# Three engines held to the order of the program in both mixers of a hybrid diffusion backbone

## The chip, the cores and the metric

One core of a Trainium2 chip runs the whole kernel in one launch. The metric is the device time of that launch in microseconds (us), lower is better. Differences of under about 0.2% (5.4 us) are not told from no change here.

## The reference

Two layers work on 512 tokens of 1024 channels: 256 context tokens and 256 latent tokens. A layer is a half-step SwiGLU, a token mixer, and a second half-step SwiGLU, each wrapped in a modulated post-norm. The mixer is what matters here:

```
p   = u @ w_in                          # z, x, B, C, dt | lx, lg | q, k, v, g, alr | gate
ssd = rms_norm(bidirectional chunked scan of (x, dt, B, C) * silu(z))
lru = (forward + backward linear scan of conv(lx)) * gelu(lg)
gla = rms_norm(bidirectional gated linear attention of (q, k, v)) * silu(g)
y   = (sum over n of sigmoid(gate_n) * (branch_n @ w_branch_n)) @ w_out
```

Latent scans start from the final context state. In layer 1 only latent tokens leave the mixer, so much of its work is on 256 columns (`c0 = TL`).

## The kernel before

**Products.** Activations lie with channels on partitions and tokens along the columns. A float32 product is made of three fp32r matmuls (`mm3`, L372 to L374): activations and weights are each split into a rounded part and a rest. A weight block of 128 x 1024 is loaded by SyncE, ScalarE writes its rounded part (L342), VectorE its rest (L344), both in `split_ahead`. One such block feeds one projection: `proj` (called a step below) issues 24 matmuls into one PSUM bank.

**Foreground and background.** `mixer` goes through two hand-written lists, `ORDER` and `ORDER2`. Their letters are foreground steps: L an LRU pair, S an SSD group (four channel tiles through `chan`, two z tiles), G a gate, M and B merges of a branch, V and Q the GLA projections, D the dt rows, N the SSD norm. The scans are background generators (`lru_batch`, `ssd_dt`, `ssd_group`, `ssd_norm`, `gla_head`). After every projection `pump` advances them by a budget of 5.0 us in layer 0 and 2.5 us in layer 1 (the numbers that they yield), and a `yield None` ends a generator's turn. `need(t)` advances the first generator in the list again and again until `t` is done.

**Chains between engines.** `chan` evicts a projection with a convolution: ScalarE L860, six (or eight) VectorE pieces L869, ScalarE tanh L1413, VectorE L1414. `ssd_group` works two heads at a time: states (L1065, L1072), decay exponents (VectorE L1088, ScalarE L1090 and L1092), state output (L1097, L1100), weights L1108, a GpSimd sum L1111, the product L1118, the rest L1124 to L1132. `ssd_norm` takes eight tiles, each VectorE L1154, ScalarE L903, VectorE L904. `gla_head` ends in L1242 (transposes), L1259 and L1263 (states), L1279 (output), L1287, L1288, L1292, L897, L898, L1298, L1300.

**Who sets the order.** What is written above is the order in which the program emits instructions. The framework then schedules them: it keeps data dependences and, on each engine, places what its own estimates call ready, earlier emitted work first. So before the change any instruction may pass another on its engine. `keep_in_program_order` (used by `pin` for the very first stage and by `table` for table preloads) adds an edge without a wait: the instruction is placed behind everything emitted before it on its engine. SyncE's and GpSimd's instructions carry no such edge before or after.

Of the kernel before, what the change touches and what calls it, by code (L numbers as in the profile page):

```python
# [39 lines left out]
ORDER2 = ("V0 Q0 N Q1 B0 B1 B2 B3 H0 V1 Q2 B4 B5 B6 H1 Q3 B7 F H2 G24 G20 G21 G22 G23 C G25 G26 G27",  # L40
          "V0 Q0 N G00 G01 G02 Q1 B0 G05 B1 V1 B2 H0 B3 Q2 B5 B4 H1 Q3 B6 B7 F H2 G22 C G20 G21 G27 G23 G24 G26 G25")
POOL_HI = (0, 0)
SEG = ((), ())
LOW = 4
BUDGET = (5.0, 2.5)
# [22 lines left out]
class Any:  # L68
    def __getattr__(self, n):
        return self  # L70
# [11 lines left out]
        return False  # L82


class Half:


    def __init__(self, page, o):
        self.page, self.o, self.mate = page, o, None
# [7 lines left out]
class Prog:  # L97
    def __init__(self, tc, aps, wlist=None, seq=None):
        self.dry = tc is None
        self.tc = Any() if self.dry else tc  # L100
        self.nc = self.tc.nc
        self.a = aps if not self.dry else Any()
        self.plan = seq
        self.seq = []
        self.wlist = wlist
# [394 lines left out]
    def prologue(self):  # L500
        nc, a = self.nc, self.a
        self.hp = [self.F() for _ in range(KT)]
        cs = self.F()
        nc.vector.memset(self.ones, 1.0)
        nc.sync.dma_start(cs[:, :16].rearrange("p (k b) -> p k b", b=2), a["cc"])
        nc.scalar.dma_start(self.par[0], a["par"][0])
        self.raw_free += self.once
        self.retired = {id(t) for t in self.once}
        for k in range(KT):
            self.ada_load(k)  # L510
            nc.sync.dma_start(self.hp[k], a["hT"][:, k])
            if not self.dry:
                self.raw_issue(min(NRAW + len(self.once), k + 1))
        nc.vector.memset(self.sst.rearrange("p a b -> p (a b)"), 0.0)
        self.filler()
        nc.scalar.activation(self.sst[:, :, 0:2], cs[:, :16].rearrange("p (k b) -> p k b", b=2), AF.Silu)
        self.fF(cs)
        if not self.dry:
            make_identity(nc, self.ident)
        srow = self.F()  # L520
        nc.vector.tensor_copy(srow[:, 0:16].rearrange("p (b k) -> p k b", b=2), self.sst[:, :, 0:2])
        ps = self.B()
        nc.tensor.transpose(ps[0:16, 0:P], srow[:, 0:16], self.ident)
        nc.scalar.activation(srow[0:16, P:2 * P], ps[0:16, 0:P], AF.Copy)
        self.fB(ps)
        nc.gpsimd.dma_start(self.s_d.rearrange("b (k p) -> (b k) p", p=P), srow[0:16, P:2 * P])
        self.fF(srow)
        nc.vector.memset(self.eps, EPS)
        nc.vector.memset(self.eps4, 4.0 * EPS)
        four = self.ident.rearrange("p (j a c) -> p j a c", a=2, c=32)  # L530
        nc.vector.tensor_tensor(self.sel.rearrange("p (j c) -> p j c", c=2), four[:, :, 0, 0:2], four[:, :, 1, 0:2],
                                op=ALU.add)
        for d in range(2):
            nc.gpsimd.memset(self.gmask[d], 1.0)
            nc.gpsimd.affine_select(out=self.gmask[d], in_=self.gmask[d], pattern=[[1 if d == 0 else -1, P]],
                                    compare_op=ALU.is_ge, fill=0.0, base=0,
                                    channel_multiplier=-1 if d == 0 else 1)
        for c in (64, 128):
            nc.vector.memset(self.rst[c], 1.0)
            nc.vector.memset(self.rst[c].rearrange("p (a b) -> p a b", b=c)[:, :, 0:1], 0.0)  # L540
# [470 lines left out]
    def ssd_group(self, l, g, ys, Bp, Cp, zs, c0):  # L1011
# [31 lines left out]
        for p in range(2):  # L1043
# [35 lines left out]
            for d in range(2):  # L1079
                for i in range(2):  # L1080
                    o = 32 * d + hh[i]
                    act = 2 * d + i in SEG[l]
                    for c in ch:
# [240 lines left out]
    def mixer(self, l):  # L1324
        nc = self.nc
# [5 lines left out]
        self.bg = []  # L1331
        self.ssq = None
        self.split_banks = True
        def gate(n, m):
            pg = self.proj(self.in_specs(l, OFF["gate"] + n * D + m * P), u, c0)
            th = self.Fc(c0)
            nc.scalar.activation(th[:, c0:], pg[:, c0:], AF.Tanh, scale=0.5)
            self.fB(pg)
            return th
# [35 lines left out]
        def merge(n, m, br, th=None):  # L1375
            th = th or eg.pop((n, m), None) or gate(n, m)
            pb = self.proj([("br", l, n, k, m) for k in range(KT)], lambda k: br[k], c0)
            nc.vector.scalar_tensor_tensor(th[:, c0:], th[:, c0:], 1.0, pb[:, c0:], op0=ALU.add, op1=ALU.mult)
            self.fB(pb)
            if m not in mp:  # L1380
                mp[m] = th
            else:
                nc.vector.tensor_tensor(mp[m][:, c0:], mp[m][:, c0:], th[:, c0:], op=ALU.add)
                self.fF(th)
# [48 lines left out]

        self.pool_hi = POOL_HI[l]
        for x in ORDER[l].split():
            i = int(x[1:] or 0)
            if x[0] == "D":
                alr, dtg = dt_rows()
            elif x[0] == "L":
                lru_pair(i)  # L1440
            elif x[0] == "S":
                ssd_start(i)
            elif x[0] == "G":
                eg[divmod(i, 10)] = gate(*divmod(i, 10))
            elif x[0] == "P":
                self.pool_hi = i
            elif x[0] == "R":
                self.need(*bt)
            elif x[0] == "M":
                merge(1, i, lru)  # L1450
# [51 lines left out]
        for x in ORDER2[l].split():  # L1502
            i = int(x[1:] or 0)
            if x[0] == "V":
                v = gla_v(i)
            elif x[0] == "Q":
                gla_proj(i, v)
            elif x[0] == "N":
                self.need(*sg)
                norm = self.start(self.ssd_norm(l, ys, c0, ssd))  # L1510
            elif x[0] == "B":
                self.need(norm)
                merge(0, i, ssd)
            elif x[0] == "H":
                self.need(gh[i])
            elif x[0] == "G":
                eg[divmod(i, 10)] = gate(*divmod(i, 10))
            elif x[0] == "F":
                for t in range(KT):
                    self.fR(*ssd[t])  # L1520
            elif x[0] == "C":
                cv = self.start(self.to_hilo(go, range(6), c0, gla))
# [4 lines left out]
        for m in range(KT):  # L1527
            merge(2, m, gla)
            x = mp[m]
# [4 lines left out]
        for t in range(KT):  # L1534
            self.fR(*gla[t])
        self.split_banks = False
        assert not self.hfree and len(self.rpages) == 2 * len(self.rpairs)
        self.more_slots([], [self.pair(self.rpairs[i:i + 2]) for i in range(0, len(self.rpairs) - 1, 2)])
        self.res_begin(l, 1, 1.0, c0)
# [201 lines left out]
```

## Time and profile before

| | |
|---|---|
| median of 3 runs | 2720.79 us (2719.93 to 2722.16) |
| profiled execution | 2721.23 us, span 2719.4 us |
| TensorE matmul, weight load | 2659.5 us (98%), 2282.7 us (84%) |
| VectorE | 1932.3 us (71%) |
| ScalarE | 1224.6 us (45%) |
| GpSimd | 349.9 us (13%) |

Busy time is the union of an engine's instructions. Ends of matmuls are modelled, so a busy TensorE need not be at its peak. The mixer of layer 0 runs from about 388 to 1209 us of the span, that of layer 1 from about 1945 to 2506 us.

### The profile page before, as it was taken

Reading aid. Unit: us, or ns where it says so; the run is one execution under the profiler, and the core shown is the slowest. Engines: PE = TensorE matmul, PEld = TensorE weight load, DVE = VectorE, ACT = ScalarE, POOL = GpSimd, SP = SyncE. Lnnn points to the kernel's source line nnn. Section 1 sums busy time; section 2 is a strip of 40 time slices with the busy share of each in tenths; the row PEclk is TensorE's granted clock in tenths of the full one; section 3 lists DMA queues with packets and bytes.
Section 4 is the critical chain, followed back from the end, with each engine's and each line's share of the span. In section 5 each row is a group of like instructions: output and inputs, shape, how many; then the busy total and the mean of one; then the engine's idle time right before and its main releaser. Section 6 shows DMA issues by size and latency. Waiting matters only on the chain.

```text
span 2719.4 us, 38650 instructions
## 1 busy us (share of the span) xinstructions
PE 2659.5 (98%) x14869; PEld 2282.7 (84%) x14869; DVE 1932.3 (71%) x3469; ACT 1224.6 (45%) x1757; POOL 349.9 (13%) x296
## 2 busy tenths in 40 slices
PE   9999999999999999999999999999999999999997
PEld 7888897677888888888888888888977898899997
DVE  5888769599986545468887587633698898676654
ACT  4233237863435444433323142332388645575543
POOL 0000132112220000040000130001311112012002
PEclk9999999999999999999999999999999999999999
DMA  7566533134342222235556435532333454343553
GB/s 287 191 189 200 176 121 125 63 100 149 123 145 74 82 86 78 86 101 170 192 193 196 132 133 186 177 117 99 105 111 108 134 173 140 102 147 125 176 190 116
DMA packets 117832, 380.48 MB, mean 140 GB/s; under 512 B 13888, under 2 KB 22352, under 8 KB 117648
## 3 DMA queue, kind: packets, MB, share of 16 engines
q1 hardware_dynamic: 116000, 373.52, 41.8%
q0 software_dynamic: 1504, 4.34, 0.5%
q8 instruction: 116, 1.90, 0.3%
q14 instruction: 68, 0.56, 0.1%
q10 hardware_dynamic: 144, 0.17, 0.0%
HBM read 373.63 MB, written 4.33 MB: 139 GB/s over the span
## 4 chain that ended last, share of the span: by engine, by line
PE 64%; DVE 7%; ACT 3%; issue 2%; DMA 1%; POOL 0%; SPq 0%; DVEq 0%; POOLq 0%; ACTq 0%
PE bank L372 20%; PE bank L373 19%; PE bank L374 19%; PE bank L1279 1%; PE bank L1259 1%; DVE x L869 1%; DVE wl L344 1%; PE bank L1097 1%; PE bank L1065 0%; PE bank L1118 0%; DVE f L669 0%; DVE m1l L344 0%; DVE f L670 0%; DVE x L1108 0%; PE bank L921 0%
## 5 line engine op out<-in xcount | busy, mean ns | idle before, releaser
L342 ACT ACTIVATE wh<-wr 128x1024 fp32r<-128x1024 f32 x388 | 410.2, 1058 | 734.3 <-PE bank L373 526.2
L344 DVE TENSOR_TENSOR wl<-wr,wh 128x1024 fp32r<-128x1024 f32 x388 | 483.5, 1247 | 257.6 <-ACT wh L342 256.2
L488 DVE SCALAR_TENSOR_TENSOR ada_scr<-wr,sb 128x1024 f32<-128x1024 f32 x256 | 316.3, 1236 | 128.6 <-DMA wr<-in_ws_dram 126.0
L372 PE MATMUL bank<-u0h,wh 128*128 128x512 f32 (+1 forms) x660 | 246.3, 375 | 5.3 <-ACT u0h L675 3.8
L372 PE MATMUL bank<-r,wh 128*128 128x512 f32 (+1 forms) x736 | 251.4, 342 | 0.0
L373 PE MATMUL bank<-r,wh 128*128 128x512 f32 (+1 forms) x736 | 249.7, 340 | 0.0
L374 PE MATMUL bank<-r,wl 128*128 128x512 f32 (+1 forms) x736 | 249.6, 339 | 0.0
L373 PE MATMUL bank<-u0l,wh 128*128 128x512 f32 (+1 forms) x660 | 236.0, 358 | 2.1 <-DVE u0l L677 2.0
L374 PE MATMUL bank<-u0h,wl 128*128 128x512 f32 (+1 forms) x660 | 237.3, 360 | 0.4 <-DVE wl L344 0.4
L372 PE MATMUL bank<-u1h,wh 128*128 128x512 f32 (+1 forms) x660 | 234.7, 358 | 0.6 <-ACT u1h L675 0.6
L373 PE MATMUL bank<-u1l,wh 128*128 128x512 f32 (+1 forms) x660 | 234.3, 356 | 0.8 <-DVE u1l L677 0.7
L374 PE MATMUL bank<-u1h,wl 128*128 128x512 f32 (+1 forms) x660 | 234.1, 355 | 0.0
L372 PE MATMUL bank<-u2h,wh 128*128 128x512 f32 (+1 forms) x660 | 233.5, 355 | 0.0
L373 PE MATMUL bank<-u2l,wh 128*128 128x512 f32 (+1 forms) x660 | 233.3, 354 | 0.0
L374 PE MATMUL bank<-u2h,wl 128*128 128x512 f32 (+1 forms) x660 | 232.8, 353 | 0.0
L373 PE MATMUL bank<-u3l,wh 128*128 128x512 f32 (+1 forms) x644 | 228.5, 355 | 1.2 <-DVE u3l L677 1.2
L372 PE MATMUL bank<-u3h,wh 128*128 128x512 f32 (+1 forms) x644 | 228.5, 356 | 0.0
L374 PE MATMUL bank<-u3h,wl 128*128 128x512 f32 (+1 forms) x644 | 228.2, 355 | 0.0
L372 PEld LDWEIGHTS bank<-r,wh 128*128 128x128 f32 x736 | 139.4, 190 | 15.3 <-ACT wh L342 0.2
L374 PEld LDWEIGHTS bank<-r,wl 128*128 128x128 f32 x736 | 139.5, 190 | 14.9
L373 PEld LDWEIGHTS bank<-r,wh 128*128 128x128 f32 x736 | 139.5, 190 | 14.8
L372 PEld LDWEIGHTS bank<-u0h,wh 128*128 128x128 f32 x660 | 125.8, 191 | 28.4 <-issue 5.7
(507 smaller groups left out, 5918.2 us busy)
## 6 DMA issues: line engine op xcount, KB each, us to landing
wr<-in_ws_dram SPq DMA_DIRECT2D x602, 512.0 KB, 3.5
m1r<-in_ws_dram SPq DMA_DIRECT2D x29, 512.0 KB, 3.9
ada<-in_ws_dram SPq DMA_DIRECT2D x16, 512.0 KB, 9.0
x<-acs_d SPq DMA_DIRECT2D x26, 256.0 KB, 3.4
x<-acs_d SPq DMA_DIRECT2D x45, 128.0 KB, 3.8
x<-in_lw_dram SPq DMA_DIRECT2D x16, 256.0 KB, 3.7
sb<-s_d SPq DMA_DIRECT2D x6, 512.0 KB, 5.8
f<-acs_d SPq DMA_DIRECT2D x19, 128.0 KB, 3.8
```

What stands on the lines that cost most here:

```text
L342: self.pin(nc.scalar.activation(hi, raw, AF.Copy))
L344: self.pin(nc.vector.tensor_tensor(lo, raw, hi, op=ALU.subtract))
L372: x = self.pin(nc.tensor.matmul(out, st[0], mv[0], start=start, stop=False, skip_group_check=True))
L373: self.pin(nc.tensor.matmul(out, st[0], mv[1], start=False, stop=False, skip_group_check=True))
L374: self.last_mm = self.pin(nc.tensor.matmul(out, st[1], mv[0], start=False, stop=stop, skip_group_check=True))
L488: nc.vector.scalar_tensor_tensor(self.ada_scr, raw.rearrange("p a b -> p (a b)"), 1.0, self.sb[b], op0=ALU.mult, op1=ALU.mult, accum_out=o ...
L869: nc.vector.scalar_tensor_tensor(ys[:, :, a:z], xs[:, :, a + o:z + o], w(k), ys[:, :, a:z], op0=ALU.mult, op1=ALU.add)
L1097: nc.tensor.matmul(cc(ps, c), cc(Sd[d], c), cc(Cp, c), start=True, stop=True, skip_group_check=True)
L1259: nc.tensor.matmul(ps[:, 0:256], cc(kt[d], a), vv(a), start=True, stop=True)
L1279: nc.tensor.matmul(cc(po[w], c), lh, rh, start=n == 0, stop=n == len(steps) - 1, skip_group_check=True)
```

## The change

Inside `mixer`, from the start of its first projection to the point ahead of the residual stage, every matmul, transpose, activation and vector operation (the names in `OPS`) is given the edge that keeps it behind whatever was emitted before it on TensorE, VectorE or ScalarE. A thin wrapper around the core's engines does this. What is emitted, its operands and its order of emission stay as they were; `ORDER`, `ORDER2` and the budgets are untouched.

```diff
+ORDERED = ("tensor", "vector", "scalar")
...
+class Engine:
...
+    OPS = {"matmul", "transpose", "activation", "tensor_tensor", "tensor_scalar", "scalar_tensor_tensor", "tensor_copy",
+           "tensor_tensor_scan", "reciprocal"}
...
+        def op(*a, **k):
+            x = f(*a, **k)
+            if self.name in self.prog.ordered:
+                self.prog.tc.keep_in_program_order(x)
+            return x
+        return op
...
-        self.nc = self.tc.nc
+        self.ordered = ()
+        self.nc = Any() if self.dry else Core(self)
...
         self.split_banks = True
+        self.ordered = ORDERED
...
         self.split_banks = False
+        self.ordered = ()
```

## Rows read from the trace of the kernel before

**Rows 1.** The page's busy time by engine over the whole span.
```profile
PE 2659.5 (98%) x14869; PEld 2282.7 (84%) x14869; DVE 1932.3 (71%) x3469; ACT 1224.6 (45%) x1757; POOL 349.9 (13%) x296
```

**Rows 2.** Busy time in three stretches (columns: stretch, length, engines, PEclk, DMA, GB/s).
```profile
388.00:514.00 126.00, 118.36 (x574) 93.26 (x573) 99.96 (x185) 92.91 (x128) 29.57 (x25) 0.97 0.32 104
514.00:765.00 251.00, 241.63 (x1188) 196.06 (x1188) 228.29 (x513) 130.08 (x192) 54.88 (x29) 0.99 0.35 115
1967.00:2281.00 314.00, 299.90 (x1812) 255.44 (x1811) 274.17 (x573) 210.86 (x333) 56.57 (x56) 0.98 0.41 133
```

**Rows 3.** TensorE's waits in mixer 0: us in total, times, longest.
```profile
PE bank L921 <- ACT x L1000: 4.9, 1, 4.9
...
PE bank L921 <- ACT x L922: 2.8, 1, 2.8
```

**Rows 4.** ScalarE by line, 514 to 765: busy, mean ns, idle before and releaser.
```profile
L342 ACT ACTIVATE wh<-wr 128x1024 fp32r<-128x1024 f32 x36 | 37.9, 1055 | 43.8 <-PE bank L373 40.5 <-issue 3.3
L1090 ACT ACTIVATE x<-x 128x512 f32<-128x512 f32 x22 | 13.8, 628 | 8.8 <-DVE x L1088 8.1
...
L1413 ACT ACTIVATE x<-x 128x512 f32<-128x512 f32 x15 | 9.4, 629 | 20.9 <-DVE x L869 20.9
...
L1092 ACT ACTIVATE x<-x 128x512 f32<-128x512 f32 x6 | 3.8, 627 | 7.1 <-DMA x<-acs_d 7.1
...
L903 ACT ACTIVATE r<-x 128x512 fp32r<-128x512 f32 x5 | 3.2, 633 | 4.9 <-DVE x L965 4.8
```

**Rows 5.** VectorE by line, 514 to 765.
```profile
L1414 DVE SCALAR_TENSOR_TENSOR x<-x,x 128x512 f32<-128x512 f32 x15 | 10.2, 683 | 0.6 <-ACT x L1413 0.6
...
L946 DVE SCALAR_TENSOR_TENSOR x<-x,x 128x512 f32<-128x512 f32 x8 | 5.3, 687 | 10.8 <-ACT x L941 10.8
...
L904 DVE TENSOR_TENSOR r<-x,r 128x512 fp32r<-128x512 f32 x5 | 3.4, 682 | 0.7 <-ACT r L903 0.7
```

**Rows 6.** Chain of waits, 733 to 757: start, us, what.
```profile
734.64 1.34 PE bank L1065 x12
...
741.43 1.34 PE bank L1097 x12
```

**Rows 7.** Timeline, 841 to 890, VectorE and then ScalarE: start, us, instruction.
```profile
866.09 2.06 DVE L1154 SCALAR_TENSOR_TENSOR x<-x,par,x 128x512 f32<-128x512 f32 x3
...
880.80 0.69 DVE L1288 TENSOR_TENSOR x<-x,x 128x512 f32<-128x512 f32 x1 [0.58 <-ACT x L1287]
...
885.52 1.28 DVE L1298 TENSOR_TENSOR x<-bank,x 128x512 f32<-128x512 f32 x2
886.72 1.40 DVE L1300 SCALAR_TENSOR_TENSOR x<-x,par,x 128x512 f32<-128x512 f32 x2
...
882.71 0.69 ACT L897 ACTIVATE x<-bank,eps 128x512 f32<-128x512 f32 x1 [0.64 <-PE bank L1292]
```

**Rows 8.** Timeline, 2281 to 2324, TensorE and then ScalarE.
```profile
2284.41 1.50 PE L1065 MATMUL bank<-x,x 128*128 128x128 f32 x12
...
2291.30 0.65 PE L1118 MATMUL bank<-x,x 128*64 128x128 f32 x6
...
2311.06 0.42 ACT L903 ACTIVATE r<-x 128x256 fp32r<-128x256 f32 x1 [0.55 <-DVE x L1154]
```

**Rows 9.** Table loads: groups of mixer 0 (370 to 1230), then one load's timeline.
```profile
L232 ACT ACT_TABLE_LOAD x9 | 11.5, 1283 | 0.2
...
L1090 ACT ACT_TABLE_LOAD x1 | 1.3, 1283 | 0.0
...
849.11 1.28 ACT L232 ACT_TABLE_LOAD   x1
850.40 1.16 ACT L1181 ACTIVATE x<-x 128x512 f32<-128x512 f32 x2
```

**Rows 10.** Granted clock (third from last) behind the longest TensorE wait of mixer 0.
```profile
468.00:471.00 3.00, 2.98 (x5) 1.75 (x6) 3.00 (x9) 2.95 (x4) 0.00 (x0) 0.50 0.90 276
471.00:474.00 3.00, 3.00 (x8) 1.81 (x8) 2.64 (x11) 2.96 (x5) 0.00 (x0) 0.61 0.39 150
```

More of the change, by code (lines that the diff above doesn't have):

```diff
@@ L82, in __exit__, with __init__, __getattr__ @@
         return False
+class Engine:
+    OPS = {"matmul", "transpose", "activation", "tensor_tensor", "tensor_scalar", "scalar_tensor_tensor", "tensor_copy",
+           "tensor_tensor_scan", "reciprocal"}
+    def __init__(self, prog, name):
+        self.prog, self.name, self.eng = prog, name, getattr(prog.tc.nc, name)
+    def __getattr__(self, n):
+        f = getattr(self.eng, n)
+        if n not in self.OPS:
+            return f
+        def op(*a, **k):
[4 more added lines that the diff above has]
+        return op
+class Core:
+    def __init__(self, prog):
+        self.nc = prog.tc.nc
+        self.tensor, self.vector, self.scalar = (Engine(prog, n) for n in ("tensor", "vector", "scalar"))
+    def __getattr__(self, n):
+        return getattr(self.nc, n)
 class Half:
@@ L518, in prologue @@
         if not self.dry:
-            make_identity(nc, self.ident)
+            make_identity(nc.nc, self.ident)
         srow = self.F()
```

## The prediction

> **What bounds the kernel now.** Read the page's busy shares first: TensorE is busy 98% of the span, VectorE 71%, ScalarE 45% [rows 1]. That is an average. The change touches the mixers alone, so take the busy times by stretch next [rows 2]. In the SSD part of layer 0 (514 to 765) VectorE works 228.3 of 251 us, in the LRU and SSD part of layer 1 (1967 to 2281) 274.2 of 314: there two engines are nearly full at once, TensorE with 9.4 and 14.1 us idle, VectorE with 22.7 and 39.8. In the LRU part of layer 0 (388 to 514) ScalarE works 92.9 of 126 and TensorE idles 7.6. Then the waits of TensorE: the two largest of layer 0 that name ScalarE are 4.9 and 2.8 us, both in LRU batches [rows 3]. Last, who waits inside the full stretch: VectorE waited 0.6 us in all for the tanh L1413 (15 of them, 0.63 us each) and 0.7 for the rounding L903 [rows 4, 5]. These chains go VectorE, ScalarE, VectorE with nothing between them in the program, so other instructions stand in their gaps now: VectorE's order in the trace is not the program's. TensorE's nearly is: between the state products L1065 and the outputs L1097 lie exactly 24 foreground matmuls, (741.43 - 734.64 - 1.34) = 5.45 us [rows 6], and I take 5.45 for a full-width step and half of it, 2.7, for a step of 256 columns.
>
> **The change part by part.** It adds no instruction and removes none but table loads. What it takes away is the filling of gaps. I went through the emission order and noted where a wait becomes bare.
>
> *1. Chains inside the full stretch of layer 0.* Each of 16 channel tiles: VectorE stands for L1413, 16 x 0.63 = 10.1 us. After it ScalarE does the next weight block, L342, 1.06, while VectorE does L1414, 0.68, and then L344 needs the block: 16 x 0.4 = 6. After a head pair's last L1088 come one L1090 and two L1092 before ScalarE can evict the next projection: 0.63 + 2 x 0.63 = 1.9, for some six pairs 11.3. Five L903, 0.63 each, 3.2 [rows 4, 5]. Together 30.6. The wait of 10.8 for the LRU exponentials stays [rows 5]. VectorE then needs 228.3 + 10.8 + 30.6 = 269.7 in 251: **+19**. Bounds: 0 if VectorE is never more than a step behind where TensorE needs it, +31 if no wait falls into today's idle time. I take the middle value since 12 of today's 22.7 us are not that LRU wait. Behind a standing L1414 are queued L344 of the block two steps on and the next convolution, whose bank and whose weights TensorE waits for.
>
> *2. The same in layer 1.* Most channel tiles are full width: 16 x 0.6 = 9.6; 16 x 0.4 = 6.4; eight pairs at two thirds of 1.9 (L903 is 0.42 on half the columns against 0.63 [rows 4, 8]), 10; eight roundings 3.4: 29.4. 274.2 + 29.4 = 303.6 would fit into 314, but load and budget are uneven: a channel step of 2.7 to 5.45 us carries a weight split, a convolution and 2.5 us of background. Bounds 0 and +29. I take **+10**, a third.
>
> *3. The drain ahead of B0, both layers.* `need(norm)` first runs `gla_head` to its end, then the norm, with no projection between. In layer 0 three norm tiles are emitted between the transposes and L1263; a tile is 0.69 + 0.63 + 0.68 = 2.0 us [rows 4, 5, 7] now that L904 cannot wait beside the next L1154. L1263 waits 6, TensorE has about 2 us of its own there: 4 lost. L1287 (as L903) and L1288 stand bare ahead of L1292: 1.3. After L1292: 0.69 + 0.63 + 1.28 + 1.40 = 4.0, then four tiles, 8.0; the gate and merge of B0 are 10.9 and hide all but 1.1 and the last block's matmuls. About **+7**. In layer 1 five tiles come after L1292, and the gate was done early: two thirds of (4.0 + 5 x 2.0) is 9.3 against a merge of 2.7: 6.6 and the small wait, **+7**. Bounds 0 and +12 each.
>
> *4. The drain at N in layer 1.* `need(*sg)` runs the last pair from L1065 to L1118 with no projection between. In the trace that takes 2284.4 to 2292.0, 7.5 us, and foreground matmuls stand in it [rows 8]. Bare, I take **+6**; bounds: half of 7.5, since about that was foreground, and 7.5. In layer 0 this pair ends before N.
>
> *5. The clock.* After the 4.9 us wait the granted clock is 0.50 for 3 us and 0.61 for the next 3, the lower level of 1.2 GHz for most of it [rows 3, 10]: 1.5 + 1.2 = 2.7 us lost behind a wait of that length. I count two to three more such waits (B0, N): **+6**; bounds -5 (today's drops go) and +12.
>
> *6. Table loads.* Layer 0 has 47 in 13 groups, 1.283 us each [rows 9]. Which functions share a table the trace shows by where no load stands. Counted so in program order there are 35, as each LRU batch then does its sigmoids, roots and exponentials in one piece: 12 x 1.283 = 15.4 us of ScalarE. Six of the 12 lie in the LRU part, where ScalarE ends waits: **-6**; bounds 0 and -15. A load costs its own length only: the next activation starts 850.40 - (849.11 + 1.28) = 0.01 us later [rows 9]. The Trainium skill (ScalarE: Activation LUTs, "What ACT_TABLE_LOAD costs") adds a drain of 1.38 us to each switch, 2.66 together. By it the 12 would give 32 us and the six 16, and the forecast would be 10 us lower; the row shows no drain, so it does not enter.
>
> Everything else I cost at nothing: GLA heads are spread over pumps with `yield None` and VectorE is half idle there; the final merges have no background; SyncE's queue is free as before. If the loads on it slip, wh comes late: two to four steps of lookahead cover that.
>
> Sum: 19 + 10 + 7 + 7 + 6 + 6 - 6 = **+49**. The profiled execution took 2721.2 us (its span 2719.4 and 1.8 around it), 0.4 above the median of the runs: **2770 us**.
>
> **The rivals.**
>
> *A. Faster.* The scheduler works from estimates; TensorE's idle time is partly its misplacement. If VectorE is always within one step of TensorE, parts 1 to 4 vanish. Then ScalarE decides, in the LRU parts: the 7.6 us idle and 3.8 us of clock (0.03 x 126) there, and half of the 14.1 in layer 1, go: -18, **2703**. For it: fewer loads, and the budgets in the program pace the background. Against: VectorE at 91% of the full stretch leaves no room for bare chains. It decides from the point where layer 0's 30.6 us fit into idle time.
>
> *B. No change.* TensorE's order is nearly the program's already [rows 6], and gains in LRU pay for the drains: **2721**. Against: bare waits are on the other two engines.
>
> *C. Lockstep.* All bare waits count, tables gain nothing, drains take their upper bounds: 30.6 + 29.4 + 24 + 7.5 + 12 = 103.5, **2825**. For it: ScalarE's tanh waits for VectorE's convolution and holds the next weight block behind it, and the background products need the pump before.
>
> *D. The order doesn't change,* since scheduled order equals program order: excluded for VectorE and ScalarE by the filled gaps [rows 5].
>
> **How the numbers follow.** Forecast 0.50, its own range 2740 to 2800; C 0.20; A 0.22; B 0.08. A measurement of this kernel tells 0.2% (5.4 us) from no change. So slower 0.70, same 0.08, faster 0.22. The range of 2708 to 2835 leaves out about half of A and a third of C.
>
> **What would show it.** L1414 waits for L1413 by about 0.6 us each in the changed trace, and L904 for L903; the eight L1154 come 2.0 us apart in layer 0. In 514 to 765 the same steps take some 270 us, with VectorE the engine that TensorE waits for. Behind B0 and at N TensorE's granted clock falls to 0.5. The LRU parts get shorter, with 35 loads in layer 0. I am wrong if TensorE's idle time in the mixers shrinks, or if the loss sits in the GLA heads, the merges or a DMA wait.

## The result and the profile after

The changed kernel takes **3006.07 us** (median of 4 runs, 3003.12 to 3008.02) against 2720.36 us before (4 runs): 285.7 us slower, ratio 1.105 (95% interval 1.1033 to 1.1060). The forecast of 2770 had the sign and a sixth of the size, and its range ended at 2835. The profiled execution has a span of 3006.3 us and a mean granted clock of 0.952 (0.992 before).

In the changed kernel a helper issues the wrapped instructions, so the trace shows them all at one line, L101; its rows are read by their tiles. `x<-bank,par 128x512` on ScalarE is L860 or L922, `x<-x` the tanh L1413 (in sums of waits also L1090, L1092 and L1132), `r<-x` the rounding L903, `wh<-wr` the split L342; on VectorE `wl<-wr,wh` is L344, the scans are L956 to L960, and `x<-bank,par,x 128x255` is the convolution. In the experiments' own rows the line numbers are those of before.

The page's busy time of the changed kernel answers to [rows 1]:

```profile
PE 2742.2 (91%) x14869; PEld 2330.8 (78%) x14869; DVE 1954.5 (65%) x3469; ACT 1203.7 (40%) x1740; POOL 316.2 (11%) x296
```

VectorE has the same instructions and ScalarE 17 fewer, all of them table loads; TensorE is busy 83 us longer with the same matmuls, and all three stand more. Next, busy time by stretch, for the stretches in which as many foreground matmuls end as in those of [rows 2] (columns: stretch, length, PE, PEld, DVE, ACT, POOL, granted clock, DMA share, GB/s):

```profile
389.50:560.00 170.50, 133.40 (x575) 100.86 (x573) 110.86 (x190) 84.73 (x117) 26.97 (x29) 0.89 0.26 81
560.00:873.50 313.50, 258.68 (x1189) 205.37 (x1188) 218.95 (x496) 126.92 (x192) 48.82 (x28) 0.89 0.28 88
2114.50:2524.50 410.00, 318.69 (x1813) 267.95 (x1813) 279.00 (x563) 204.92 (x327) 51.58 (x56) 0.87 0.31 100
```

These three are 44.5, 62.5 and 96.0 us longer than before, 203 of the 286 us. TensorE's idle time there rose from 7.6, 9.4 and 14.1 us to 37.1, 54.8 and 91.3, together by 152; its busy time for the same matmuls rose by 15.0, 17.0 and 18.8 us, together 51, and the granted clock fell from between 0.97 and 0.99 to between 0.87 and 0.89. Counted by foreground matmuls done, 16 us more go where layer 1's mixer starts (in what were the 32 us ahead of the third stretch), and 66 us behind the LRU and SSD lists (24 in layer 0, 42 in layer 1).

TensorE's waits in mixer 0 (us in total, times, longest) answer to [rows 3], where the two largest that named ScalarE were 4.9 and 2.8:

```profile
PE bank L101 <- ACT x L101: 52.1, 5, 20.2
PE bank L101 <- DVE x L101: 19.4, 8, 8.0
PE bank L101 <- ACT wh L101: 14.9, 6, 5.1
PE bank L101 <- DVE wl L101: 11.5, 7, 7.0
```

One stand in the timeline shows how it comes about. TensorE first (start, us, instruction, idle time before it and releaser): six rows of LRU gate products (L921), 14.87 us of nothing, the next two.

```profile
604.81 2.73 PE L101 MATMUL bank<-x,x 128*128 128x512 f32 x6
622.41 2.08 PE L101 MATMUL bank<-x,x 128*128 128x512 f32 x2 [14.87 <-ACT x L101]
```

ScalarE in the same time:

```profile
602.04 0.76 ACT L101 ACTIVATE x<-bank,par 128x512 f32<-128x512 f32 x1
608.11 0.63 ACT L101 ACTIVATE x<-x 128x512 f32<-128x512 f32 x1 [5.30 <-issue]
608.64 1.04 ACT L101 ACTIVATE wh<-wr 128x1024 fp32r<-128x1024 f32 x1
614.42 0.63 ACT L101 ACTIVATE r<-x 128x512 fp32r<-128x512 f32 x1 [4.74 <-DVE x L101]
614.96 0.76 ACT L101 ACTIVATE x<-bank,par 128x512 f32<-128x512 f32 x1
618.78 0.63 ACT L101 ACTIVATE x<-x 128x512 f32<-128x512 f32 x1 [3.06 <-DVE x L101]
619.32 1.04 ACT L101 ACTIVATE wh<-wr 128x1024 fp32r<-128x1024 f32 x1
620.38 1.28 ACT L101 ACT_TABLE_LOAD   x1
621.67 1.84 ACT L101 ACTIVATE x<-bank,par 128x512 f32<-128x512 f32 x3
```

And VectorE, a convolution and then one turn of it:

```profile
605.12 2.91 DVE L101 SCALAR_TENSOR_TENSOR x<-bank,par,x 128x255 f32<-128x255 f32 x6
608.77 0.69 DVE L101 SCALAR_TENSOR_TENSOR x<-x,x 128x512 f32<-128x512 f32 x1 [0.74 <-ACT x L101]
609.71 1.23 DVE L101 TENSOR_TENSOR wl<-wr,wh 128x1024 fp32r<-128x1024 f32 x1 [0.26 <-ACT wh L101]
610.86 0.68 DVE L101 TENSOR_TENSOR_SCAN x<-x,x 128x256 f32<-128x256 f32 x1
611.58 0.75 DVE L101 TENSOR_TENSOR_SCAN x<-x,x,x 128x256 f32<-128x256 f32 x1
613.70 0.69 DVE L101 TENSOR_TENSOR x<-x,x 128x512 f32<-128x512 f32 x1 [1.37 <-POOL x L996]
615.09 0.69 DVE L101 TENSOR_TENSOR r<-x,r 128x512 fp32r<-128x512 f32 x1 [0.69 <-ACT r L101]
615.75 2.94 DVE L101 SCALAR_TENSOR_TENSOR x<-bank,par,x 128x255 f32<-128x255 f32 x6
619.45 0.69 DVE L101 SCALAR_TENSOR_TENSOR x<-x,x 128x512 f32<-128x512 f32 x1 [0.76 <-ACT x L101]
```

The background has three PSUM banks, and the fourth product needs one of them back. The sigmoid that empties the first one (L922, 621.67) stands in ScalarE's queue behind two tanh, a rounding and two weight splits, and ScalarE waited 5.30, 4.74 and 3.06 us there for VectorE (the first row names no releaser, but its tanh starts at 608.11, and the convolution that it reads ends at 605.12 + 2.91 = 608.03). VectorE meanwhile takes 10.7 us for one turn (608.77 to 619.45): the background that one pump emits, and one channel's split and convolution. One projection of TensorE is 5.45 us [rows 6]. Before the change such a turn's background could lie where VectorE had room; now every later weight block waits for it. The Trainium skill (PSUM — Partial Sum Buffer, "Engine vs sequencer instructions") calls the queues of ScalarE, VectorE and GpSimd strict FIFO and has matmuls start in program order; these rows agree for ScalarE, VectorE and TensorE: nothing passes a standing instruction.

Last, whom ScalarE waits for. Before, from 388 to 765:

```profile
ACT wh L342 <- PE bank L373: 48.7, 25, 4.2
ACT x L1413 <- DVE x L869: 20.9, 10, 8.8
ACT x L1132 <- DVE x L1131: 15.7, 3, 7.6
ACT r L903 <- DVE x L965: 13.5, 5, 3.4
ACT x L1090 <- DVE x L1088: 8.1, 9, 2.0
```

After, in the same work, 389 to 873:

```profile
ACT x L101 <- DVE x L101: 101.2, 30, 8.2
ACT x L101 <- PE bank L101: 64.6, 35, 8.2
ACT r L101 <- DVE x L101: 56.4, 8, 13.1
...
ACT wh L101 <- PE bank L101: 6.6, 3, 3.7
```

Before, ScalarE's largest wait was for TensorE to give a weight slot back: it was ahead with the weights. Of these 48.7 us 6.6 are left: the lead in weight blocks is gone. Its waits for VectorE at `x` and `r` are as many as before, 38 against 37, but came to 157.6 us against 67.4. It also stands 64.6 us for background products of TensorE (8.8 before), so the engines hold one another, and not VectorE alone the other two.

### The profile page after: what moved, and what is told of

It is laid out like the page before. It is cut to its first block, busy times and chain, and to the rows that moved or that the text cites. A ratio compares the mean times of both kernels' runs of the same rounds, so it can differ in the third digit from the quotient of the medians.

```text
span 3006.3 us, 38551 instructions
## 1 busy us (share of the span) xinstructions
PE 2742.2 (91%) x14869; PEld 2330.8 (78%) x14869; DVE 1954.5 (65%) x3469; ACT 1203.7 (40%) x1740; POOL 316.2 (11%) x296
## 3 DMA queue, kind: packets, MB, share of 16 engines
q0 software_dynamic: 1504, 4.34, 0.5%
## 5 line engine op out<-in xcount | busy, mean ns | idle before, releaser
L101 DVE TENSOR_TENSOR wl<-wr,wh 128x1024 fp32r<-128x1024 f32 x388 | 480.1, 1238 | 229.4 <-ACT wh L101 228.3
L101 ACT ACTIVATE wh<-wr 128x1024 fp32r<-128x1024 f32 x388 | 409.3, 1056 | 511.8 <-PE bank L101 396.6
L101 DVE SCALAR_TENSOR_TENSOR ada_scr<-wr,sb 128x1024 f32<-128x1024 f32 x256 | 315.9, 1234 | 134.6 <-DMA wr<-in_ws_dram 131.2
L101 PE MATMUL bank<-r,wh 128*128 128x512 f32 (+1 forms) x1472 | 376.1, 346 | 5.4 <-ACT r L101 4.7
L101 PE MATMUL bank<-x,x 128*128 128x128 f32 (+4 forms) x1018 | 195.1, 353 | 140.7 <-ACT x L101 90.0
L101 PEld LDWEIGHTS bank<-r,wh 128*128 128x128 f32 x1472 | 258.7, 193 | 39.5 <-ACT r L101 6.9
L101 PEld LDWEIGHTS bank<-x,x 128*128 128x128 f32 (+1 forms) x1018 | 130.3, 193 | 191.2 <-ACT x L101 100.2
L101 PE MATMUL bank<-u0h,wh 128*128 128x512 f32 (+1 forms) x660 | 253.4, 385 | 21.6 <-ACT wh L101 14.9
L101 PE MATMUL bank<-u0h,wl 128*128 128x512 f32 (+1 forms) x660 | 242.4, 367 | 12.1 <-DVE wl L101 11.8
L101 PE MATMUL bank<-r,wl 128*128 128x512 f32 (+1 forms) x736 | 251.6, 342 | 0.0
L101 PE MATMUL bank<-u1h,wh 128*128 128x512 f32 (+1 forms) x660 | 238.7, 363 | 5.1 <-ACT u1h L101 5.1
L101 PE MATMUL bank<-u0l,wh 128*128 128x512 f32 (+1 forms) x660 | 241.2, 365 | 1.5 <-DVE u0l L101 1.1
L101 PE MATMUL bank<-u1l,wh 128*128 128x512 f32 (+1 forms) x660 | 238.7, 362 | 1.3 <-DVE u1l L101 0.8
L101 PE MATMUL bank<-u2h,wh 128*128 128x512 f32 (+1 forms) x660 | 235.5, 358 | 3.1 <-ACT u2h L101 3.1
L101 PE MATMUL bank<-u1h,wl 128*128 128x512 f32 (+1 forms) x660 | 236.6, 359 | 0.0
L101 PE MATMUL bank<-u2l,wh 128*128 128x512 f32 (+1 forms) x660 | 234.8, 356 | 0.5
L101 PE MATMUL bank<-u2h,wl 128*128 128x512 f32 (+1 forms) x660 | 233.6, 354 | 0.0
L101 PE MATMUL bank<-u3l,wh 128*128 128x512 f32 (+1 forms) x644 | 228.8, 356 | 1.5 <-DVE u3l L101 0.9
L101 PE MATMUL bank<-u3h,wh 128*128 128x512 f32 (+1 forms) x644 | 228.4, 356 | 0.0
L101 PE MATMUL bank<-u3h,wl 128*128 128x512 f32 (+1 forms) x644 | 228.0, 354 | 0.0
L101 ACT ACTIVATE x<-x 128x512 f32<-128x512 f32 (+2 forms) x218 | 119.1, 573 | 215.6 <-DVE x L101 200.4
L101 ACT ACTIVATE x<-bank 128x512 f32<-128x512 f32 (+3 forms) x218 | 96.5, 471 | 194.2 <-PE bank L101 181.8
```

The source lines that it names most:

```text
L101: x = f(*a, **k)
```

## The experiments

All were timed against the kernel before on the same chip; "+" is the difference from before's median of the same group of runs, to compare with **+286** for the full change. Each difference is known to about 4 us.

**One engine, two engines.** The edit is the tuple of engines that keep program order:

```diff
-ORDERED = ("tensor", "vector", "scalar")
+ORDERED = ("tensor",)            # only_tensor
+ORDERED = ("vector",)            # only_vector
+ORDERED = ("scalar",)            # only_scalar
+ORDERED = ("tensor", "vector")   # scalar_free
+ORDERED = ("vector", "scalar")   # tensor_free
```

The first theory (S) came from the timeline above: ScalarE's queue holds the banks.

> Only TensorE keeps program order in the mixers; VectorE and ScalarE are scheduled freely as before. Theory (S): the 285 us come from ScalarE's order: a copy that frees a background PSUM bank stands behind ScalarE instructions that wait for VectorE's backlog. Here that coupling is gone, so 2710 to 2760 us. Rival (T): TensorE itself, which may no longer put the next projection's matmuls into a gap, carries the loss: over 2850 us. Rival (V), VectorE's bare chains: 2715 to 2740, since VectorE is free.

> Only VectorE keeps program order. Theory (S): 2720 to 2780 us, some bare chains of 0.6 us each, but TensorE and ScalarE fill in. Rival (V): the bare chains make VectorE the bound of the stretches where it worked 228 of 251 and 274 of 314 us: over 2850 us. Rival (T): no change, 2715 to 2740.

> Only ScalarE keeps program order. Theory (S): bank copies again stand behind the LRU roundings and the tanh, but VectorE can bring forward what ScalarE waits for and TensorE can go on with projections: 2760 to 2850 us, the dearest of the three single engines. Rival (T) and rival (V): within 20 us of before, 2715 to 2740; fewer table loads could even give 2700.

> TensorE and VectorE keep program order, ScalarE does not. Theory (S): most of the loss is gone, 2740 to 2820 us, and the waits of over 10 us of TensorE for a bank are gone. Rival (V) or (T): at least 2900 us, since the engine that carries the loss is still held.

Measured: TensorE alone 2774.96 (+55), VectorE alone 2851.01 (+131), ScalarE alone 2802.18 (+82), TensorE with VectorE 2914.62 (+195). (S) falls: without ScalarE's order 195 of 286 us remain, and VectorE's is the dearest. The single-engine rivals fall too: TensorE alone stays far below the 2850 of (T), and (V), whose figures came out where VectorE was held (over 2850, at least 2900), wanted at most 2740 for each of the other two alone. What stands out is the sum: 55 + 131 = 186 against 195, and all three 268 against 286. That gave theory (Q), own losses that add, and a number for the next pair.

> VectorE and ScalarE keep program order, TensorE does not. The three single engines added 55 + 131 + 82 = 268 of the 285 us, so the theory is now (Q): each held engine has its own loss, since an instruction that the program asks for too early stands at the head of its queue until another engine delivers, and all behind it stand too; the losses add. Then 2720 + 131 + 82 = 2933, 2910 to 2955 us. Rival (S), the first theory: bank copies that stand in ScalarE's queue hold TensorE; a free TensorE goes on with projections, so at most 2870 us.

Measured 2938.69 (+218; the sum was 213). (Q) named 2933 ahead of the run; (S) wanted 2870 at most.

**The weight split.** The two instructions of the split are issued without the edge, so they may pass a standing one:

```diff
-                self.pin(nc.scalar.activation(hi, raw, AF.Copy))
+                self.pin(nc.nc.scalar.activation(hi, raw, AF.Copy))          # L342: splits_free, l342_free
-            self.pin(nc.vector.tensor_tensor(lo, raw, hi, op=ALU.subtract))
+            self.pin(nc.nc.vector.tensor_tensor(lo, raw, hi, op=ALU.subtract))  # L344: splits_free, vector_split_free
```

> All three engines keep program order, but the two instructions of the weight split (L342, L344) have no edge: they may pass a standing instruction. (Q): the splits are only one of the things queued behind a standing instruction. TensorE stood for foreground matmuls 45 of some 230 us of its waits in both mixers, so 30 to 80 us come back: 2925 to 2975. Rival (W), the prediction's own picture that TensorE waits mostly since the weight splits and convolutions behind a standing VectorE come late: more than 150 us come back, below 2855. Rival (S): 2990 to 3010, no change.

> As splits_free, but only ScalarE's half of the split (L342) has no edge; VectorE's half (L344) keeps program order. Theory (R), the ring: ScalarE stands at a rounding L903 or a tanh L1413 for VectorE, the next L342 is queued behind it, and VectorE then stands at L344 for that L342 (156 us of VectorE's waits in both mixers), so the two take turns. A free L342 breaks the ring: at least 100 of the 125 us that splits_free gave come back, 2870 to 2905 us. Rival: VectorE's half is what must pass (TensorE waits for wl): at most 40 us come back, 2965 to 3010.

> Only VectorE keeps program order, and its half of the weight split (L344) has no edge. If VectorE's 131 us are mostly weight blocks queued behind a standing VectorE instruction, at least 65 come back: 2735 to 2785 us. Rival: they are its background chains, which reach TensorE through banks and inputs of background products: at most 30 come back, 2820 to 2855.

Measured: splits_free 2881.61 (+161), 125 us back: more than (Q)'s 30 to 80, less than the 150 of (W). l342_free 2953.22 (+231), 54 back and not 100: both halves count, and (R) is half right. With VectorE alone held, vector_split_free 2779.80 (+61): 70 of VectorE's 131 us are its half of the weight split queued behind other work. Two instructions of a projection thus carry 44% of the loss (125 of 286). In splits_free ScalarE is ahead with the weights again (389 to 800, beside 48.7 before and 6.6 after):

```profile
ACT wh L342 <- PE bank L373: 60.3, 23, 5.0
```

**Emission with distance.** `yield None` ends a background's turn, so a projection comes between producer and consumer; the tanh is emitted behind the next projection.

```diff
-        n = 0
+        n = 0; yield None                          # ahead of L946: lru946, lru_gap, skew
...
-            yield 1.4
+            yield 1.4; yield None                  # ahead of L965: lru_gap, skew
-            nc.vector.tensor_tensor(tf[:, c0:], tf[:, c0:], gl[:, c0:], op=ALU.mult)
+            nc.vector.tensor_tensor(tf[:, c0:], tf[:, c0:], gl[:, c0:], op=ALU.mult); yield None   # ahead of L903: lru903, lru_gap, skew
...
-            t = self.Fc(lo)
-            nc.scalar.activation(t[:, lo:], y[:, lo:], AF.Tanh)
...
+            late.append((y, lo)); return y         # tanh and L1414 behind the next proj: tanh_late, skew
```

skew also adds turns ahead of L994, L1034, L1097, L1118 and L1132; skew_splits is skew with the free splits.

> All three keep program order; in the LRU background three turns end earlier (a yield None ahead of L946, ahead of the gelu product L965 and ahead of its rounding L903), so that a foreground projection lies between a producer and its consumer on another engine. (Q): the stands of 10 to 20 us at L946 and behind L903 shrink; about half of the 92 us that layer 0 loses up to the second SSD group and some in layer 1 come back: 2900 to 2965 us. Rival (C), the loss is VectorE's and ScalarE's capacity in these stretches and not the distance: 2990 to 3030, or worse, since LRU ends later and its last part falls into a drain.

> All three keep program order, of the three later turns of lru_gap only the one ahead of L946, where VectorE stood 50 us in the changed kernel for ScalarE's LRU exponentials. If this stand carries lru_gap's 63 us: 2945 to 2970. If the rounding L903 behind the gelu product carries it: 2985 to 3010.

> All three keep program order; of the three later turns of lru_gap only the one between the gelu product L965 and its rounding L903. If a rounding that ScalarE meets while VectorE is still scans behind is what holds the next weight block, 40 to 65 us come back: 2940 to 2965. If the 63 us came from spreading the LRU over more projections, whichever the place, none comes back from one turn, as in lru946: 2990 to 3010.

> All three keep program order; the tanh L1413 and L1414 of a channel tile are emitted behind the next projection and its background, the LRU as in the changed kernel. If the standing tanh holds the next weight block, 30 to 70 us come back: 2935 to 2975. If VectorE's backlog is what is late, ScalarE only stands a step later: 2985 to 3010.

> All three keep program order; the LRU turns of the run before, and the same in the SSD background (ahead of L1034, L1097, L1118, L1132 and L994), and each channel's tanh L1413 and L1414 are emitted behind the next projection. (Q): distance in the program is the cause, so most of the loss goes: 2760 to 2880 us. Rival (C): at least 2970 us, since no work is taken from any engine.

> All three held, with both the later turns of skew and the free splits of splits_free. If they take away different waits, both gains add: 3006 - 101 - 125 = 2780, 2760 to 2810 us. If both only shorten the same stands of VectorE and ScalarE, the larger one and a little: 2850 to 2880.

Measured: lru_gap 2942.90 (+222), 63 back; lru946 3005.67 (+287), none; lru903 2965.49 (+246), 39 back, just under its 40 to 65; tanh_late 2968.92 (+250), 36 back; skew 2905.36 (+185), 101 back, far from the 126 to 246 expected; skew_splits 2848.05 (+126).

So a turn ahead of L946, where VectorE stood longest, gives nothing back; before the change it stood 26.0 us there in layer 0 too (3 times, longest 15.2). The stand did not go away but moved: in lru946 VectorE waits for ScalarE up to 19.9 us at L344, 15.9 at L869 and 17.0 at L876, in this part of layer 0 127 us in all against 131 in the changed kernel. The two ScalarE instructions that wait for VectorE's queue do cost, as the rows below show for tanh_late and lru903 (389 to 860): each run shortens its own stand, to 23.2 us in the first (L1413 is now at L1415) and to 19.9 in the second, and leaves the other's.

```profile
ACT r L903 <- DVE x L965: 76.4, 8, 13.1
...
ACT x L1415 <- DVE x L869: 23.2, 7, 7.5
```

```profile
ACT x L1413 <- DVE x L869: 78.9, 15, 8.5
...
ACT r L903 <- DVE x L965: 19.9, 3, 9.1
```

lru_gap's 63 and tanh_late's 36 make 99, and skew gave 101: in the total the SSD turns are worth nothing. Counted by foreground matmuls done they do help where they stand: of some 200 us lost in the three stretches lru_gap leaves 141, tanh_late 164 and skew 75. But the background that skew puts off has to end ahead of B0, and the second lists lose 88 us with it against 66, most of that in layer 0 (32 against 13 from 841 to 890 of the time before). Distance in the program thus gives back over half of what the first lists lose, and a third in all. With the free splits 160 of the 226 come back that the two would give if they added: they partly shorten the same stands.

**A fourth bank.**

```diff
-NBG = 3
+NBG = 4
```

> All three held, background products have four PSUM banks in place of three. In the changed kernel TensorE stood 87.9 us for a bank at L1034 and L921, 12 us of mean clock loss beside it. (S): without these waits 60 to 100 us come back: 2905 to 2945. (Q) and (R): ScalarE's and VectorE's queues are as late as before and TensorE meets them at its next product: 2970 to 3010.

Measured 2992.94 (+271), 15 back, as (Q) had it. The waits at L1034 and L921 are nearly gone (10.6 us in both mixers), and TensorE meets the same lateness at the weights (its waits in mixer 0):

```profile
PE bank L372 <- ACT wh L342: 31.8, 10, 9.3
PE bank L374 <- DVE wl L344: 14.7, 11, 7.0
...
PE bank L921 <- ACT x L922: 6.9, 2, 5.1
```

The 20.2 us at a bank, the most striking row of the trace, were in the main where the delay showed and not its cause. One thing blurs this: the fourth bank is taken from the foreground, which keeps four of the eight, and TensorE now waits 16.2 us (4 times) at L372 for the convolution L869 to empty a bank, as it never does in the changed kernel. What a bank without this price would give was not run.

**The second list alone.** The order starts between the two lists:

```diff
-        self.split_banks = True; self.ordered = ORDERED
+        self.split_banks = True
...
+        v = norm = cv = None; self.ordered = ORDERED
```

> All three keep program order only from the point between the two lists on (GLA projections, the SSD norm, the merges); the LRU and SSD lists are scheduled freely. In the changed kernel this part lost 24 us in layer 0 and 42 us in layer 1. If the drains there cost by themselves: 2775 to 2800 us. If they were late because of what was lost ahead: 2730 to 2755; the prediction's parts 3 to 5 come to 26 us, 2747.

Measured 2784.92 (+66), what this part had lost in the full change (24 + 42), so the second list costs by itself. By foreground matmuls done, in both kernels, 37 us of it lie where the drains are (13 from 841 to 890 of the time before, 24 from 2281 to 2324) and some 30 behind them, among GLA heads and merges. The row is the drain at N in layer 1; the changed kernel has the same wait, to the hundredth:

```profile
2314.80 0.69 PE L1118 MATMUL bank<-x,x 128*64 128x128 f32 x2 [4.34 <-POOL x L1111]
```

**Without any order.**

```diff
-ORDERED = ("tensor", "vector", "scalar")
+ORDERED = ()      # before_skew: emission of skew; before_lru_chan: LRU turns and late tanh only
```

> No engine is held, as before; the emission is that of skew. If distance in the program matters only to engines that are held, no change: 2705 to 2735 us. If the scheduler too gains from it, below 2705; if the later end of the background costs (the wait ahead of B0 was 18 us longer in skew), above 2735.

> No engine is held; the LRU turns and the later tanh of skew, without its SSD turns. In before_skew TensorE was 18 us ahead of before by the end of layer 0's SSD list and 7 us ahead at the same place of layer 1, and lost it again where the SSD turns end later. Without them 2695 to 2712 us, a little faster than before. Rival: the gain came from the SSD turns, or the scheduler gives it back elsewhere: 2714 to 2730.

Measured: before_skew 2719.24 against 2721.96, ratio 0.9992 (0.9983 to 1.0001), no change. before_lru_chan **2707.88** against 2718.84, ratio **0.9961 (0.9948 to 0.9975)**, 11 us faster than the kernel before and the fastest of all (5 of its 6 runs within 2705.43 to 2708.10, one at 2718.61). The gain is in layer 0, where the bank waits of [rows 3] are gone: by foreground matmuls done it is 7 us ahead at 514 of the time before and 11 at 765. Its LRU stretch (columns as above):

```profile
388.00:514.00 126.00, 124.42 (x607) 98.09 (x606) 103.12 (x180) 97.58 (x134) 32.56 (x28) 1.00 0.31 108
```

TensorE gets 607 matmuls into these 126 us, where it had 574 before [rows 2].

## Why the prediction was wrong

**The step that failed** is the one costed at nothing: "Everything else I cost at nothing", and behind it "If the loads on it slip, wh comes late: two to four steps of lookahead cover that". The loads did not slip (ScalarE waited 42.3 us in all for the loads of weight blocks, 58.5 before); the splits did, since they are in the same queues as everything else. Their lead is what program order used up (48.7 us of ScalarE waiting for slots down to 6.6), and letting only the two splits pass gives 125 us back.

**Parts 1 and 2** (+19 and +10) priced a bare wait right and looked at the wrong engine. VectorE stands 0.74 us for the tanh and 0.69 for the rounding, as forecast. But ScalarE's own stands were not priced: 4.1 us each (157.6 in 38) against 0.63, as long as VectorE's backlog. And the sum of 269.7 us in 251 was an average over a stretch, while a queue in program order pays turn by turn: 10.7 us of VectorE against 5.45 of TensorE. VectorE did not become the full engine that this sum made of it; it works 219 of the 313.5 us there. Measured: +62.5 and +96.0, and 16 at the start of layer 1. How much of it would go with a smaller background budget per projection was not tried.

**Part 6** had the count nearly right and the effect wrong. Layer 0 has 36 loads where 35 were counted (groups 389 to 1342 of the changed kernel):

```profile
L101 ACT ACT_TABLE_LOAD x27 | 34.6, 1283 | 7.5 <-PE bank L101 7.1
...
L265 ACT ACT_TABLE_LOAD x9 | 11.5, 1283 | 0.2
```

The LRU part got 44.5 us longer all the same and not 6 shorter: ScalarE, busy 84.7 of the 170.5 us, is not what bounds it. The load at 620.38 above ends at 621.66, and the next activation starts at 621.67. The Trainium skill (ScalarE: Activation LUTs, "What ACT_TABLE_LOAD costs") adds a drain of 1.38 us to each switch; these rows show none, neither behind the load nor ahead of it (the split before it ends at 620.36).

**Parts 3 and 4** (7 + 7 + 6) had the mechanism. The norm tiles of layer 0 come 2.05 us apart (2.0 forecast):

```profile
979.00 0.75 DVE L101 SCALAR_TENSOR_TENSOR x<-x,par,x 128x512 f32<-128x512 f32 x1
...
981.05 0.75 DVE L101 SCALAR_TENSOR_TENSOR x<-x,par,x 128x512 f32<-128x512 f32 x1
...
983.11 0.74 DVE L101 SCALAR_TENSOR_TENSOR x<-x,par,x 128x512 f32<-128x512 f32 x1
```

The state products beside L1263 waited 5.5 us (4 forecast), L1292 1.4 (1.3). At N, TensorE's waits sum to 7.1 us (1.66, 0.27, 4.34, 0.84) against a term of 6. But the stretches of the drains lost 37 us against these 20; matmuls behind a stand ran at the lower clock there, which may be the rest. The other 30 of the 66 us of second_half lie among GLA heads and merges, which the prediction cost at nothing (L1214 waits 10.8 us, 7 times); by its own words a loss there counts against it, though it is a tenth of the whole.

**Part 5**, the clock, +6 within -5 to +12, was mis-sized: most of the 51 us more of TensorE's busy time in the three stretches is this term. TensorE worked 108 us at the lower level there against 22 before; as half of that is lost, my estimate is 43 us. Behind the 14.87 us stand (clock third from last):

```profile
616.00:619.00 3.00, 0.00 (x0) 0.00 (x0) 2.55 (x6) 0.22 (x1) 0.00 (x0) 0.50 0.00 0
622.00:625.00 3.00, 2.59 (x4) 1.46 (x5) 0.00 (x0) 1.99 (x4) 1.26 (x1) 0.50 0.56 175
625.00:628.00 3.00, 3.00 (x13) 2.38 (x13) 1.92 (x2) 1.65 (x3) 1.29 (x1) 0.88 0.02 5
```

By the forecast's own reckoning this stand cost 1.5 + 0.4 = 1.9 us, less than the 2.7 forecast; but TensorE stood 17 times for over 3 us in these stretches, against 3 before, where two or three more had been counted.

**The rivals.** C, lockstep, was the mechanism: it names the tanh that holds the next weight block and the products that need the pump before. At 2825 it added up every bare wait at its own length and so missed that a wait grows with the queue ahead of it. A and B are out, and D too.

## What to carry to other kernels

When an engine is held to program order, price a wait by the queue of the engine that is waited for, not by the one instruction that releases it, and do it for every held engine, also one that is busy 45% of the time. Look first for the instruction that feeds the bottleneck from inside that queue (here the weight split): its lead is lost first, and leaving it out of the order gave back more than any other edit tried on the full change. A long wait of the bottleneck names the place where a delay shows; one more buffer there, taken from another use, moved it and gave back 15 of 286 us.

## What was not expected of the hardware

The losses of the three queues nearly add (55, 131 and 82 make 268; together they cost 286), where a chain of waits would have let one hide another. Behind a stand of 14.87 us TensorE's granted clock was 0.50 for 3 us and 0.88 for the next 3; TensorE's longer busy time, most of it from such drops, made about a quarter (51 of 203 us) of the loss in the three stretches.

Open: the 24 us between lru903 and lru_gap, of which the turn ahead of L965 was not run alone; TensorE with ScalarE held, the third pair; and the 126 us that remain in skew_splits, of which by foreground matmuls done 76 lie in the second lists and 36 in the three stretches.
